# Forming two of the four weight sums of a seven-product pair by a DMA that adds in place, in a two-layer encoder on one core

## The chip, the core and the metric

The kernel runs on one core of a Trainium2 chip. A core has a matrix engine (PE, with PEld for its weight loads), a vector engine (DVE), an activation engine (ACT), a general engine (POOL), an engine that only issues transfers (SP), and 16 DMA engines that move data between the chip's main memory (HBM) and the on-chip buffer (SBUF). The five engines run their own instruction lists in order and wait for each other by semaphores. The metric is the device time of one execution in microseconds (us), lower being better, and it is quoted as the median of several runs.

## What is computed

Two layers of an encoder over 512 tokens of width 1024. Each layer has three parts, and every part adds to x:

```python
for l in range(DEPTH):                       # DEPTH = 2
    x = x + hybrid_mixer(rms_norm(x, ...), w_in[l], ...)          # two kinds of attention heads
    x = x + memory_cross_attention(rms_norm(x, ...), rms_norm(mem, ...), ...)
    x = x + conv_ffn(rms_norm(x, norm_ffn[l]), w_up[l], conv_w[l], conv_b[l], w_down[l])
return rms_norm(x, norm_final)

def conv_ffn(h, w_up, conv_w, conv_b, w_down):
    u = h @ w_up                             # 1024 -> 2 * 2816: a gate half and a value half
    ...                                      # width-3 depthwise convolution over positions
    gate, val = jnp.split(u, 2, axis=-1)
    return (jax.nn.silu(gate) * val) @ w_down
```

The change lies in `h @ w_up`.

## The kernel before, in words

**Numbers in two parts.** Every fp32 operand of a product is split into a rounded part (hi) and a rest (lo), and a product is three matmuls: hi·hi, hi·lo, lo·hi. ACT makes hi by a cast (`ACT.copy`), and POOL or DVE makes lo by a subtraction (`tensor_sub`). `operand_of` (L566) does this for one piece of a weight, 128 partitions by 512 columns.

**Seven products for eight.** The 22 column blocks of the gate half and the 22 of the value half belong together in 22 pairs. For pairs 7 to 21 of each layer, 30 pairs in all, the product of the 2x2 blocks is formed with seven block products in place of eight (`up`, L1604). The weight's blocks are 11, 12, 21 and 22, each 128 x 512 here: raw block A of the plan holds 11 (its first half) and 22 (its second half), raw block B holds 21 and 12. The seven left operands are 11, 12, 22 and four sums, which `combined` (L576) makes:

- s1 = 22 + 21 and s3 = 11 + 21, from the raw blocks;
- s2 = s3 + 22 and s4 = s2 + 12.

Each sum is one POOL `tensor_add` of 512 columns into a temporary `t`, and then one ACT cast and one DVE subtraction into a `hi` or `lo` weight tile. A `hi`-tagged tile here holds both parts of s1 or of s4, and a `lo`-tagged one both parts of s2 or of s3. The three plain blocks go into `r` tiles, also by one cast and one subtraction each. `up` uses the operands in the order 11, s1, 22 of the pair before, s2, 12, s4, s3. Between two pairs, `down_grouped` (L1672) takes one block of the down projection: 24 matmuls of 512 columns. The products of a pair are 84 matmuls of 256 columns.

**Loads.** All weights lie in HBM in the order of use. `emit_raw` (L563) has SP load the next block of 512 KB into one of three `raw` tiles; `get_w` keeps the loading and splitting ahead of the use.

**Buffers.** `wpool` holds the raw tiles and four tiles each of `hi` and `lo`. `tpool` holds 14 temporaries `t` of 2 KB per partition, which all stages share: softmax rows, rotary pieces, convolution outputs, sums of weights.

**Who sets the order.** The calls are not issued where they are written. They are recorded on a tape (`Taped`, `Tape`), and `Tape.plan` (L375) works out an order for each engine from a table of assumed costs (`Step`, L101), the buffers there are, and the order in which the calls were recorded. `Tape.play` then issues the calls (L404, which is why the profile puts nearly every instruction on that line). The planner lets a tile of a tag be opened ahead of those recorded before it only while more than a certain number of that tag's buffers are free: for `t` that number is 9 (`ASIDE`, L77, and `room`, L292). A DMA counts as 450 ns on the engine that issues it (L117).

**The first microseconds.** SP loads x and the first three weight blocks piece by piece, then three blocks of 512 KB (raw_114 to raw_116), two bias tables, the parameters, and then pieces of the memory tokens and further blocks. POOL makes the lo parts of raw_114, raw_116 and raw_122 there, DVE those of raw_115 and raw_119; between them POOL computes the inverse root of the first norm (`s_132`) and spreads it (`s_133`). PE needs `s_133` for a small matmul (`tr_139`) and the parts of raw_119 and raw_122 for the value projection (`mm_159`, `mm_160`).

Of the kernel before, what the change touches and what calls it, by code (L numbers as in the profile page):

```python
# [11 lines left out]
F32 = mybir.dt.float32  # L12
F32R = mybir.dt.float32r
AF = mybir.ActivationFunctionType
ALU = mybir.AluOpType
# [4 lines left out]
P = 128  # L20
# [6 lines left out]
KC = D // P  # L27
# [471 lines left out]
def encoder_kernel(ctx: ExitStack, tc: tile.TileContext, t: dict, out: list):  # L499
    nc = tc.nc  # L500
    tape = Tape()
    PE, ACT, DVE, POOL, SP = (
        Taped(tape, e, calls) for e, calls in zip(ENGINES, (nc.tensor, nc.scalar, nc.vector, nc.gpsimd, nc.sync)))
    late = Late(PE)
    LO_A, SUMS, LO_S = DVE, POOL, DVE
# [2 lines left out]
    xpool = ctx.enter_context(tc.tile_pool(name="xpool", bufs=1))  # L508
    wpool = ctx.enter_context(tc.tile_pool(name="wpool", bufs=N_W))
    rpool = ctx.enter_context(tc.tile_pool(name="rpool", bufs=23))  # L510
    tpool = ctx.enter_context(tc.tile_pool(name="tpool", bufs=14))
    spool = ctx.enter_context(tc.tile_pool(name="spool", bufs=24))
    psum = ctx.enter_context(tc.tile_pool(name="psum", bufs=2, space=PSUM))

# [2 lines left out]
    def nm(s):  # L517
        uid[0] += 1
        return f"{s}_{uid[0]}"

    def rtile(shape, dt=F32R):
        return rpool.tile([P, *shape], dt, tag="r", name=nm("r"), padded_shape=[P, *pad(shape)])

    def pad(shape):
        n = 1
        for s in shape[1:]:
            n *= s
        return [1024 // n, *shape[1:]]
# [6 lines left out]
    def tmp(shape=(S,)):  # L535
        return tpool.tile([P, *shape], F32, tag="t", name=nm("t"))
# [10 lines left out]
    f = lambda ap: ap.bitcast(F32)  # L547


    plan, raws, ready = [], [], []  # L550
# [3 lines left out]
    def raw_tile():  # L554
        key, src, nk, ncol, eng = plan[len(raws)]
        if eng[1:] == "x":
            raw = rtile((nk, ncol), F32)
        else:
            raw = wpool.tile([P, nk, ncol], F32, tag="raw", name=nm("raw"), bufs=N_RAW)
        raws.append(raw)  # L560
        return raw, src

    def emit_raw():  # L563
        SP.dma_start(*raw_tile())

    def operand_of(v, tile, sub):  # L566

        w = tile.rearrange("p (n k) c -> p n k c", n=2)
        ACT.copy(w[:, 0], v)
        sub.tensor_sub(w[:, 1], v, f(w[:, 0]))  # L570
        return [(w[:, 0, k], w[:, 1, k]) for k in range(4)]

    def wtile(tag):
        return wpool.tile([P, KC, P], F32R, tag=tag, name=nm(tag))

    def combined(first, second, early):  # L576

        parts = {}
        for n, v in (("11", first[:, 0:4]), ("12", second[:, 4:8]), ("22", first[:, 4:8])):
            parts[n] = operand_of(v, rtile((8, P)), LO_A)  # L580
        sums = {n: tmp((4, P)) for n in ("s3", "s1", "s2", "s4")}
        SUMS.tensor_add(sums["s1"], first[:, 4:8], second[:, 0:4])
        SUMS.tensor_add(sums["s3"], first[:, 0:4], second[:, 0:4])
        SUMS.tensor_add(sums["s2"], sums["s3"], first[:, 4:8])
        SUMS.tensor_add(sums["s4"], sums["s2"], second[:, 4:8])
        for n, tag in (("s1", "hi"), ("s2", "lo"), ("s4", "hi"), ("s3", "lo")):
            parts[n] = operand_of(sums[n], rtile((8, P)) if early else wtile(tag), LO_S)
        return parts

    def emit_split(act=ACT, cuts=2):  # L590
        n = len(ready)
        key, src, nk, ncol, eng = plan[n]
        raw = raws[n]
        if eng == "A":
            ready.append(raw)
            return
        if eng[0] == "B":
            ready.append(combined(raws[n - 1], raw, eng[1:] == "r"))
            raws[n - 1] = raws[n] = None
            return  # L600
        raws[n] = None
        if key[0] in ("up", "down", "memq", "memo"):
            cuts = 1
        if eng[1:] == "r":
            hi, lo = rtile((nk, ncol)), rtile((nk, ncol))
        else:
            hi = wpool.tile([P, nk, ncol], F32R, tag="hi", name=nm("hi"))
            lo = wpool.tile([P, nk, ncol], F32R, tag="lo", name=nm("lo"))
        for i in range(cuts):
            k = slice(nk * i // cuts, nk * (i + 1) // cuts)  # L610
            act.copy(hi[:, k], raw[:, k])
            (POOL if eng[0] == "P" else DVE).tensor_sub(lo[:, k], raw[:, k], f(hi)[:, k])
        ready.append((hi, lo))

    def get_w(key, ahead=AHEAD):
        n = done[0]
        assert plan[n][0] == key, (plan[n][0], key)
        ahead = n + 1 + ahead
        while ahead < min(len(plan), n + 1 + AHEAD_HELD) and plan[ahead][4][1:] == "r":
            ahead += 1  # L620
        while len(ready) < min(len(plan), ahead):
            while len(raws) < min(len(plan), len(ready) + N_RAW):
                emit_raw()
            emit_split()
        while len(raws) < min(len(plan), len(ready) + N_RAW):
            emit_raw()
        done[0] += 1
        w = ready[n]
        ready[n] = None
        return w  # L630
# [34 lines left out]
    first = nc.const_aps.tensor(0.0, (P, P), F32)  # L665
# [221 lines left out]
    for n in FIRST:  # L887
        if isinstance(n, (int, slice)):
            c, cs = (n, slice(0, S)) if isinstance(n, int) else (0, n)
            hi, lo, g = nn.hi[:, c, cs], nn.lo[:, c, cs], xg0[c][:, S : S + 1]  # L890
# [7 lines left out]
        k = slice(k0, k0 + nk)  # L898
# [12 lines left out]
    for l in range(DEPTH):  # L911
# [119 lines left out]
        parts = [None] * 8  # L1031
# [935 lines left out]
```

## Time and profile before

| | |
|---|---|
| median of 3 runs | 1303.92 us (1303.55 to 1304.28) |
| the profiled execution's own time | 1303.15 us |
| its span, first to last instruction | 1301.1 us |
| mean granted TensorE clock | 0.999 |
| PE busy | 1291.9 us, 99% of the span |
| DVE, ACT, POOL busy | 1066.1, 777.3, 655.8 us |
| DMA | 137.47 MB, a mean of 106 GB/s |

The span is what the profile covers; the execution's own time has 2.05 us more, which lie around it. A matmul's row in the profile lasts longer than the time until the next one starts, since matmuls overlap, so a PE that is busy all the time isn't shown to be at its peak by that alone: the distance between the starts of equal groups tells it. In the rows, `t<-raw,raw x2` is a group of two instructions that write a `t` tile from two `raw` tiles; the profile leaves the buffers' numbers out. "Idle before" is the idle time of the engine just before, with what ended it.

### The profile page before, as it was taken

What the parts mean: (1) busy time and instruction counts of PE and PEld (TensorE: products, weight loads), DVE (VectorE), ACT (ScalarE), POOL (GpSimd) and SP (SyncE); (2) the same over time, 40 slices, a digit from 0 to 9 for tenths busy, and PEclk for the clock granted to TensorE, in tenths of its full rate; (3) what the DMA queues carried; (4) which work ended last, traced back from release to release, by engine and by line L of the source; (5) the groups of instructions that cost most, each with busy time, mean ns of one, the idle gap of its engine ahead of it and who ended that gap; (6) DMA issues with size and microseconds to landing.
All of it is one profiled execution on the core that took longest, in us unless ns stands there. A gap on an engine that the chain in (4) does not pass through costs nothing.

```text
span 1301.1 us, 20672 instructions
## 1 busy us (share of the span) xinstructions
PE 1291.9 (99%) x7485; PEld 1135.6 (87%) x7485; DVE 1066.1 (82%) x1999; ACT 777.3 (60%) x1510; POOL 655.8 (50%) x523
## 2 busy tenths in 40 slices
PE   9999999999999999999999999999999999999998
PEld 8898888888889999999888988888888999999997
DVE  8679886768999998878655887866789998997784
ACT  7776686555565555555537867865655645554552
POOL 4565866716743334334626566765367224542260
PEclk9999999999999999999999999999999999999999
DMA  8651313313323333233356322232133233333231
GB/s 286 194 171 49 114 49 97 96 35 113 98 81 98 110 134 98 66 97 113 122 162 179 114 81 82 66 99 96 49 98 97 82 113 115 112 99 98 77 118 65
DMA packets 42901, 137.47 MB, mean 106 GB/s; under 512 B 5040, under 2 KB 8496, under 8 KB 42800
## 3 DMA queue, kind: packets, MB, share of 16 engines
q1 hardware_dynamic: 42224, 135.51, 33.3%
q8 instruction: 59, 0.97, 0.3%
q10 hardware_dynamic: 576, 0.66, 0.1%
q14 instruction: 42, 0.34, 0.1%
HBM read 126.18 MB, written 2.10 MB: 99 GB/s over the span
## 4 chain that ended last, share of the span: by engine, by line
PE 94%; POOL 1%; DVE 1%; issue 1%; ACT 1%; DMA 0%; SPq 0%; DVEq 0%; POOLq 0%
PE mm L404 55%; PE sc L404 20%; PE tr L404 20%; POOL lo L404 1%; ACT t L404 0%; POOL s L404 0%; DVE t L404 0%; DVE r L404 0%; DVE s L404 0%; DMA xT<-in_w 0%; ACT r L404 0%; POOL t L404 0%; DVE mm L404 0%; DVE sc L404 0%; POOL r L404 0%
## 5 line engine op out<-in xcount | busy, mean ns | idle before, releaser
L404 POOL TENSOR_TENSOR lo<-raw,hi 128x512 fp32r<-128x512 f32 (+2 forms) x168 | 265.8, 1599 | 185.8 <-ACT hi L404 179.9
L404 PE MATMUL mm<-xg,hi 128*128 128x512 f32 (+1 forms) x1026 | 319.3, 391 | 0.0
L404 POOL TENSOR_TENSOR t<-raw,raw 128x512 f32<-128x512 f32 x60 | 86.5, 1463 | 290.4 <-DMA raw<-in_w 213.8
L404 ACT CAST hi<-raw 128x512 fp32r<-128x512 f32 (+2 forms) x216 | 163.8, 784 | 111.8 <-PE mm L404 35.2
L404 PEld LDWEIGHTS mm<-xg,hi 128*128 128x128 f32 x1026 | 188.4, 188 | 35.5
L404 PE MATMUL mm<-xg,lo 128*128 128x512 f32 (+1 forms) x513 | 199.7, 389 | 0.0
L404 PE MATMUL mm<-r,hi 128*128 128x512 f32 (+1 forms) x608 | 192.0, 388 | 0.0
L404 PE MATMUL sc<-r,r 128*128 128x256 f32 (+1 forms) x736 | 131.8, 310 | 0.9 <-ACT t L404 0.9
L404 PEld LDWEIGHTS mm<-r,hi 128*128 128x128 f32 x608 | 111.9, 188 | 21.6 <-DVE xg L404 0.8
L404 PE MATMUL mm<-r,lo 128*128 128x512 f32 (+1 forms) x336 | 123.3, 367 | 0.0
L404 PEld LDWEIGHTS mm<-xg,lo 128*128 128x128 f32 x513 | 96.3, 188 | 20.2
L404 PEld LDWEIGHTS sc<-r,r 128*128 128x128 f32 x736 | 103.5, 191 | 7.4 <-ACT t L404 2.0
L404 PE MATMUL mm<-hi,xg 128*128 128x512 f32 (+1 forms) x384 | 108.1, 358 | 0.0
L404 PE MATMUL sc<-r,hi 128*128 128x256 f32 (+1 forms) x752 | 106.7, 288 | 0.0
L404 POOL TENSOR_SCALAR t<-t,s 128x512 f32<-128x512 f32 (+1 forms) x112 | 67.0, 613 | 71.8 <-DVE s L404 71.7
L404 POOL TENSOR_TENSOR t<-t,raw 128x512 f32<-128x512 f32 x60 | 99.5, 1658 | 4.7
L404 PEld LDWEIGHTS sc<-r,hi 128*128 128x128 f32 x752 | 97.0, 192 | 1.4
L404 PE MATMUL tr<-r,lo 128*128 128x256 f32 x720 | 96.2, 283 | 0.0
L404 PE MATMUL tr<-r,r 128*128 128x256 f32 x720 | 96.1, 283 | 0.0
L404 PEld LDWEIGHTS tr<-r,r 128*128 128x128 f32 x720 | 92.6, 191 | 2.3
L404 PEld LDWEIGHTS tr<-r,lo 128*128 128x128 f32 x720 | 90.7, 192 | 0.0
L404 ACT ACTIVATE t<-sc,s,s 128x512 f32<-128x512 f32 (+1 forms) x96 | 68.1, 711 | 29.2 <-DVE s L404 25.8
(158 smaller groups left out, 2756.3 us busy)
## 6 DMA issues: line engine op xcount, KB each, us to landing
raw<-in_w SPq DMA_DIRECT2D x207, 512.0 KB, 3.6
r<-r SPq DMA_DIRECT2D x30, 256.0 KB, 3.6
r<-in_bias SPq DMA_DIRECT2D x16, 384.0 KB, 4.6
raw<-in_w SPq DMA_DIRECT2D x8, 384.0 KB, 3.8
r<-in_memT SPq DMA_DIRECT2D x4, 512.0 KB, 7.2
xT<-in_w SPq DMA_DIRECT2D x7, 256.5 KB, 4.6
r<-in_w SPq DMA_DIRECT2D x9, 128.0 KB, 4.1
t<-in_memT SPq DMA_DIRECT2D x4, 256.0 KB, 6.1
```

Source lines behind the costliest of these rows:

```text
L404: call(*args, **kwargs)
```

## The change

The temporaries shrink from 14 to 10, and the space (8 KB per partition) holds two new tiles `acc` of 4 KB. For each pair, SP loads block A (11 and 22) from HBM a second time, into `acc`. Then POOL issues a DMA with `accum_op=ALU.add`, which reads block 21 from HBM twice and adds it to both halves of `acc`. After it `acc` holds s3 and s1. ACT casts the whole tile in one instruction of 1024 columns, DVE subtracts in one of 1024; s2 and s4 are still POOL's adds, s2 now from `acc`. The weight tiles are as many as before: one `hi` and one `lo` tile for s3 and s1 together, one `hi` for s2, one `lo` for s4.

```diff
-    tpool = ctx.enter_context(tc.tile_pool(name="tpool", bufs=14))
+    tpool = ctx.enter_context(tc.tile_pool(name="tpool", bufs=10))
...
+    accs = {}
+
     def emit_raw():
+        n = len(raws)
         SP.dma_start(*raw_tile())
+        if plan[n][4] == "B":
+            accs[n] = acc = wpool.tile([P, KC, P], F32, tag="acc", name=nm("acc"), bufs=2)
+            SP.dma_start(acc, plan[n - 1][1])
+            more = plan[n][1][:, 0:4].rearrange("p k c -> p (k c)").unsqueeze(1).to_broadcast([P, 2, 4 * P])
+            POOL.dma_start(acc.rearrange("p (n k) c -> p n (k c)", n=2), more, accum_op=ALU.add)
...
-    def combined(first, second, early):
+    def combined(first, second, acc):
...
-        sums = {n: tmp((4, P)) for n in ("s3", "s1", "s2", "s4")}
-        SUMS.tensor_add(sums["s1"], first[:, 4:8], second[:, 0:4])
-        SUMS.tensor_add(sums["s3"], first[:, 0:4], second[:, 0:4])
-        SUMS.tensor_add(sums["s2"], sums["s3"], first[:, 4:8])
-        SUMS.tensor_add(sums["s4"], sums["s2"], second[:, 4:8])
-        for n, tag in (("s1", "hi"), ("s2", "lo"), ("s4", "hi"), ("s3", "lo")):
-            parts[n] = operand_of(sums[n], rtile((8, P)) if early else wtile(tag), LO_S)
+        hi, lo = wtile("hi"), wtile("lo")
+        ACT.copy(hi, acc)
+        LO_S.tensor_sub(lo, acc, f(hi))
+        for i, n in enumerate(("s3", "s1")):
+            parts[n] = [(hi[:, 4 * i + k], lo[:, 4 * i + k]) for k in range(4)]
+        s2, s4 = tmp((4, P)), tmp((4, P))
+        SUMS.tensor_add(s2, acc[:, 0:4], first[:, 4:8])
+        SUMS.tensor_add(s4, s2, second[:, 4:8])
+        for n, v, tag in (("s2", s2, "hi"), ("s4", s4, "lo")):
+            parts[n] = operand_of(v, wtile(tag), LO_S)
         return parts
```

Since the planner orders everything anew, the change shows far from its own lines. Three places follow.

On POOL near the start of the program, before the change (rows 11 to 17; `lo_135` is the lo part of raw_116, `t_161` gathers squares of the memory tokens, `s_132` and `s_133` are the first norm's root and its spread form, `lo_150` is the lo part of raw_122):

```order
11 L404 TENSOR_TENSOR lo_118<-raw_114,hi_117 128x512 x2
12 L404 TENSOR_TENSOR lo_135<-raw_116,hi_134 128x512 x2
13 L404 TENSOR_TENSOR t_161<-t_161,t_171 128x512
14 L404 TENSOR_TENSOR s_132<-s_131,mhalf 128x4
15 L404 TENSOR_TENSOR s_133<-s_132,mask 128x16
16 L404 TENSOR_TENSOR t_161<-t_161,t_189 128x512
17 L404 TENSOR_TENSOR lo_150<-raw_122,hi_149 128x512 x2
```

and there now (`acc_838` and `acc_858` belong to the first two pairs, which PE multiplies some 350 us later):

```order
11 L404 TENSOR_TENSOR lo_118<-raw_114,hi_117 128x512 x2
12 L404 TENSOR_TENSOR lo_135<-raw_116,hi_134 128x512 x2
13 L404 DMA acc_838<-in_w 128x2x512
14 L404 DMA acc_858<-in_w 128x2x512
15 L404 TENSOR_TENSOR s_132<-s_131,mhalf 128x4
16 L404 TENSOR_TENSOR s_133<-s_132,mask 128x16
17 L404 TENSOR_TENSOR lo_150<-raw_122,hi_149 128x512 x2
```

Two DMA issues stand where one add stood ahead of `s_132`, and the add between `s_133` and `lo_150` has gone to a later place.

On SP at the same time, before (rows 30 to 35):

```order
30 L404 DMA gcol<-in_gcol 128x8
31 L404 DMA t_161<-in_memT 128x512
32 L404 DMA t_171<-in_memT 128x512
33 L404 DMA raw_119<-in_w 128x1024
34 L404 DMA t_189<-in_memT 128x512
35 L404 DMA raw_122<-in_w 128x1024
```

and now:

```order
30 L404 DMA gcol<-in_gcol 128x8
31 L404 DMA acc_838<-in_w 128x1024
32 L404 DMA acc_858<-in_w 128x1024
33 L404 DMA raw_119<-in_w 128x1024
34 L404 DMA t_161<-in_memT 128x512
35 L404 DMA raw_122<-in_w 128x1024
```

Ahead of raw_122 stand two loads of 512 KB in place of two of 256 KB; `t_171` and `t_189` are loaded later.

On PE, the first use of `lo_150` (a piece of the difference, - before and + now; `mm_159` and `mm_160` are two outputs of the value projection):

```order
 L404 MATMUL mm_159<-hi_149,xg_97 128x512
-L404 MATMUL mm_160<-hi_120,xg_97 128x512
-L404 MATMUL mm_160<-lo_121,xg_97 128x512
 L404 MATMUL mm_159<-lo_150,xg_97 128x512
 L404 MATMUL mm_159<-hi_149,xg_98 128x512
 L404 MATMUL mm_159<-hi_149,xg_97 128x512
-L404 MATMUL mm_160<-hi_120,xg_98 128x512
 L404 MATMUL mm_160<-hi_120,xg_97 128x512
 L404 MATMUL mm_159<-lo_150,xg_97 128x512
```

The first use of `lo_150` has come two matmuls nearer, since the two that stood ahead of it now follow. The small matmul `tr_139<-s_133,sel` likewise stands two matmuls earlier than before.

More of the change, by code (lines that the diff above doesn't have):

```diff
@@ L597, in emit_split @@
         if eng[0] == "B":
-            ready.append(combined(raws[n - 1], raw, eng[1:] == "r"))
+            ready.append(combined(raws[n - 1], raw, accs.pop(n)))
             raws[n - 1] = raws[n] = None
```

## The prediction

> **What bounds the kernel now.** I read the page first: busy times, transfer sizes, and the shares of the chain of work that ended last.
>
> ```profile
> span 1301.1 us, 20672 instructions
> PE 1291.9 (99%) x7485; PEld 1135.6 (87%) x7485; DVE 1066.1 (82%) x1999; ACT 777.3 (60%) x1510; POOL 655.8 (50%) x523
> ...
> PE 94%; POOL 1%; DVE 1%; issue 1%; ACT 1%; DMA 0%; SPq 0%; DVEq 0%; POOLq 0%
> ```
>
> PE is idle for 9.2 us of the span, and the chain runs through PE for 94% of it. POOL, which loses work by the change, is busy half the time and holds 1% of the chain. So I asked for busy time by stage: the first microseconds, the stage of the pairs (400 to 620 in the first layer), and the end.
>
> ```profile
> core 0: us, PE busy (x) PEld busy (x) DVE busy (x) ACT busy (x) POOL busy (x), PEclk, DMA share, GB/s
> 16.00:20.00 4.00, 4.00 (x19) 3.34 (x18) 3.44 (x7) 3.36 (x7) 1.00 (x1) 1.00 0.97 374
> 20.00:24.00 4.00, 4.00 (x19) 3.30 (x19) 3.94 (x4) 2.19 (x4) 4.00 (x3) 1.00 1.02 360
> 24.00:28.00 4.00, 4.00 (x20) 3.12 (x19) 3.69 (x11) 2.26 (x4) 3.45 (x4) 1.00 0.93 325
> 400.00:620.00 220.00, 220.00 (x1499) 205.04 (x1498) 195.86 (x309) 114.59 (x199) 83.09 (x54) 1.00 0.34 107
> 1250.00:1301.00 51.00, 45.20 (x313) 41.70 (x312) 29.95 (x69) 19.63 (x36) 16.29 (x10) 0.97 0.27 93
> ```
>
> Of the 9.2 us idle, 5.8 (51.00 less 45.20) lie in the last 51 us, which the change leaves as it was. 3.4 are left for everything else, and none lie in the pairs. Since busy is not yet peak, I measured the distance between equal places in neighbouring pairs, by the timeline of PE, with a stretch of single matmuls of 512 columns beside it.
>
> ```profile
> 33.84 0.39 PE L404 MATMUL mm<-lo,xg 128*128 128x512 f32 x1
> 34.07 0.39 PE L404 MATMUL mm<-hi,xg 128*128 128x512 f32 x1
> 34.30 0.39 PE L404 MATMUL mm<-lo,xg 128*128 128x512 f32 x1
> 34.52 0.62 PE L404 MATMUL mm<-hi,xg 128*128 128x512 f32 x2
> ...
> 506.18 0.63 PE L404 MATMUL mm<-xg,hi 128*128 128x512 f32 x2
> 513.08 1.60 PE L404 MATMUL sc<-r,hi 128*128 128x256 f32 x12
> 521.72 0.63 PE L404 MATMUL mm<-xg,hi 128*128 128x512 f32 x2
> 528.62 1.60 PE L404 MATMUL sc<-r,hi 128*128 128x256 f32 x12
> ```
>
> Three starts take 0.68 us, 0.227 for a matmul of 512 columns. A pair's period is 521.72 - 506.18 = 15.54 us, and the next place gives the same (528.62 - 513.08). It holds 24 matmuls of 512 columns (5.4 us) and 84 of 256 (10.1 us, 0.120 each, about half of 0.227). PE is at its pace there; nothing that other engines save can shorten it.
>
> **The change part by part.**
>
> *The pairs' sums.* The same pair on POOL and DVE, and then the groups of the stage:
>
> ```profile
> 503.95 2.87 POOL L404 TENSOR_TENSOR t<-raw,raw 128x512 f32<-128x512 f32 x2 [8.69 <-DVE t L404]
> 506.90 3.86 POOL L404 TENSOR_TENSOR t<-t,raw 128x512 f32<-128x512 f32 x2
> ...
> 513.21 0.68 DVE L404 TENSOR_TENSOR hi<-t,hi 128x512 fp32r<-128x512 f32 x1
> ```
>
> ```profile
> L404 POOL TENSOR_TENSOR t<-t,raw 128x512 f32<-128x512 f32 x26 | 43.4, 1669 | 2.0
> L404 POOL TENSOR_TENSOR t<-raw,raw 128x512 f32<-128x512 f32 x24 | 33.2, 1403 | 123.6 <-DMA raw<-in_w 80.7 <-DVE t L404 17.4 <-ACT t L404 11.3
> L404 DVE TENSOR_TENSOR hi<-t,hi 128x512 fp32r<-128x512 f32 x26 | 20.5, 789 | 1.8 <-ACT hi L404 1.8
> L404 DVE TENSOR_TENSOR lo<-raw,hi 128x1024 fp32r<-128x1024 f32 x14 | 19.5, 1391 | 0.0
> L404 DVE TENSOR_TENSOR lo<-t,lo 128x512 fp32r<-128x512 f32 x26 | 19.2, 743 | 0.0
> L404 ACT CAST hi<-t 128x512 fp32r<-128x512 f32 x25 | 15.5, 620 | 13.8 <-PE mm L404 11.1 <-POOL t L404 2.4 <-PE sc L404 0.3
> L404 ACT CAST hi<-raw 128x1024 fp32r<-128x1024 f32 x14 | 14.7, 1049 | 7.9 <-PE sc L404 7.2 <-DMA raw<-in_w 0.5
> ```
>
> Per pair POOL loses two adds of 1.40 us and keeps two (s2, s4) of 1.67, ACT exchanges two casts of 0.62 for one of 1.05, and DVE exchanges 0.79 + 0.74 for one of 1.39. That frees 2.8, 0.2 and 0.1 us. All of it is worth nothing: s1 is added from 503.95 on, its lo part is done at 513.89, and PE takes it at 528.62, 14.7 us later.
>
> *The pairs' transfers.* A pair loads 1.05 MB now and 2.10 MB after. At the 107 GB/s for a share of 0.34 above, 15.54 us move 1.66 MB; 1.05 more make the share 0.34 x 2.71/1.66 = 0.56. There is room. The accumulate's length is in no row of this kernel. Its lower bound is a plain load of 512 KB, 3.6 us here, its upper bound the same twice (the tile read and written), 7.2:
>
> ```profile
> raw<-in_w SPq DMA_DIRECT2D x207, 512.0 KB, 3.6
> ```
>
> I take 3.6, since its bytes from HBM are those of that row. Either lies inside the lead of s1 and s3: the tiles acc are two, so one is open about two periods (31 us) ahead of use, of which the base takes 4, and cast and subtraction with their queues some 7 (503.95 to 513.89 with the adds left out). About 20 us are left, so the pairs cost 0 at either bound. Issuing it on POOL is in no row; bounds are an issue of nothing and the 2.2 us after which POOL's saving of 2.8 would be nearly gone. I take 1 us, near POOL's smallest operation below (1.03); POOL is idle for more than half of the stage (83.09 of 220), so this costs 0 too.
>
> *The start.* Here something does stand close to its use. SP's issues and the times to landing of gcol (what the bases will stand behind) and of raw_122, the first of the four blocks issued from 24.69 on; then POOL, ACT and PE:
>
> ```profile
> 16.63 0.44 SPq L404 DMA_DIRECT2D gcol<-in_gcol  x1
> 24.69 8.47 SPq L404 DMA_DIRECT2D raw<-in_w  x4
> ...
> gcol<-in_gcol SPq DMA_DIRECT2D x1, 4.0 KB, 7.3
> ...
> raw<-in_w SPq DMA_DIRECT2D x1, 512.0 KB, 4.8
> ```
>
> ```profile
> 27.62 1.03 POOL L404 TENSOR_TENSOR s<-s,mhalf 128x4 f32<-128x4 f32 x1
> 28.73 0.31 POOL L404 TENSOR_TENSOR s<-s,mask 128x16 f32<-128x16 f32 x1
> 29.00 1.29 POOL L404 TENSOR_TENSOR t<-t,t 128x512 f32<-128x512 f32 x1
> 30.25 2.55 POOL L404 TENSOR_TENSOR lo<-raw,hi 128x512 fp32r<-128x512 f32 x2
> ...
> 27.00 1.14 ACT L404 CAST hi<-raw 128x512 fp32r<-128x512 f32 x2 [0.71 <-DMA raw<-in_w]
> 29.56 1.14 ACT L404 CAST hi<-raw 128x512 fp32r<-128x512 f32 x2 [0.88 <-PE mm L404]
> ...
> 29.52 0.29 PE L404 MATMUL tr<-s,sel 128*128 128x16 f32 x2
> 32.48 0.62 PE L404 MATMUL mm<-lo,xg 128*128 128x512 f32 x2
> ```
>
> raw_122 is issued at 24.69 and lands at 29.5. From its landing the first half of `lo_150` takes 2.07 us (landed 29.46, cast from 29.56, subtracted from 30.25 in 1.28, done at 31.53). PE's first use is the second matmul at 32.48, so 32.71; two matmuls earlier, as the change orders it, 32.25. The second half comes 1.28 later than the first and is used four matmuls (0.91) later, so it adds 0.37 to whatever the first half stalls.
>
> Now the loads. The DMA engines are at a share of 0.93 to 1.02 from 16 to 28 us, so a byte put ahead of raw_122 delays it. Two bases of 0.52 MB come in and two token pieces of 0.26 go later: +0.52 MB at the three windows' mean of 353 GB/s is 1.5 us, a landing at 31.0. gcol lands at 23.9 (16.63 + 7.3), the bases behind it at about 25.4 and 26.9. The two accumulates (1.05 MB, 3.0 us) are issued from POOL then, so while raw_119 and raw_122 are in flight. If they run wholly behind these, raw_122 lands at 31.0; if they are wholly served first, at 34.0; if two queues with data under way share evenly, half of the 3.0 us falls on raw_122, 32.5. I take the middle, since nothing in the trace prefers one queue. The stalls are then landing + 2.07 - 32.25 + 0.37: 1.2 us at 31.0, **2.7 at 32.5**, 4.2 at 34.0.
>
> [...] No run so far shows two such queues here.
>
> raw_119, 1.5 us late as well, is cast from 27.00 on (28.5 then), and PE takes it seven matmuls (1.6 us) ahead of `lo_150`, at 30.7 at the earliest: it holds. POOL's two issues replace an add of 1.29 ahead of `s_132`; with 1 us each `s_133` ends 0.7 later, at 29.7, while `tr_139` would come at 29.07, 0.03 after the old end of 29.04. That stall, 0.7 us, lies in the same wait as the larger one (PE then reaches `lo_150` later by just as much), so it adds nothing. If both issues took the upper 2.2 us it would be 3.1 and would replace the 2.7.
>
> *Ten temporaries for fourteen.* No row says what it costs; the planner has ordered the attention stages anew. PE's idle time outside the end is 3.4 us, so a better order gains at most that; I take the same as the bound of a loss, and 0 as the value, since the products are the same and PE stays the bound.
>
> *Sum.* 0 (pairs) + 2.7 (start) + 0 (attention) = +2.7 us. The profiled execution took 1303.15 us, its span 1301.1 and 2.05 around it: 1305.9. Against the median of the runs, 1303.92: **1306.6 us**.
>
> **The rivals.**
>
> - *The start hides it (not slower).* The accumulates stand behind the loads already queued and raw_122 lands at 31.0: +1.2, 1305.1. For it: the bases land only at 25.4 and 26.9, after raw_122 has been issued at 24.69. Against it: the share near 1.0. It decides when raw_122 lands before 31.5.
> - *A better order (faster).* `lo_150` isn't late, since the accumulates wait for bases that are themselves late, and the new order of attention, with the start's small waits, wins the 3.4 us: 1300.5. For it: PE's waits outside the end exist. Against it: no part of the change aims at them.
> - *The accumulate moves its bytes twice.* Then raw_122 lands at 34.0, +4.2: 1308.1. [...]
> - *The accumulate becomes the wait in the pairs (slower).* Rows of 2 KB added in place could be slow. Up to 20 us to landing it is hidden; at 25 us, seven times the 3.6 of a plain load, a tile acc is taken for 4 + 25 + 2.4 (cast and subtraction) and some 3 of queueing, 34.4 us, while two pairs need 31.1: (34.4 - 31.1)/2 = 1.65 us a pair, and for the 28 pairs after the first of each layer +46, 1350. For it: no such transfer has been seen here; against it: seven times.
> - *The change doesn't relieve POOL.* An issue of 2.2 us or more leaves POOL no freer than before. This changes nothing in the pairs, and at the start it is the 3.1 above: 1307.0, inside the forecast.
>
> **How the numbers follow.** A measurement of this kernel can tell about 0.2%, 2.6 us, from no change: faster means below 1301.3, slower above 1306.5. The forecast (raw_122 between 31.5 and 33.3, attention within 1 us) has 0.35; its centre lies on the edge, so 0.19 of it count as slower and 0.16 as the same. The hidden start has 0.25, the same. The better order has 0.17, faster; the bytes twice 0.14, slower; the wait in the pairs 0.09, slower. That makes faster 0.17, same 0.41, slower 0.42. The range leaves out the wait in the pairs (0.09) and half of the better order beyond its 3.4 (0.08): from 1300.5 (1303.92 - 3.4) to 1311.5 (1303.92 + 4.2 + 3.4).
>
> **What the changed profile would show.** Right: in the pairs a period of 15.54 us as before with DMA at about 0.56, POOL's `t<-raw,raw` gone; raw_122 to landing at 31.5 to 33.3 us; a PE idle of about 2.7 us between 29 and 36 released by POOL's `lo`; PE busy unchanged within 1 us, and its idle grown by 2 to 3. Wrong: a longer period or PE waits on `acc` in 400 to 620 (the wait in the pairs), no PE idle near 32 (the hidden start), or more than 2 us lost or won in 60 to 290 or 680 to 930 (the attention).

## The result and the profile after

| | before | after |
|---|---|---|
| median of 4 runs | 1303.82 us | 1319.78 us (1318.69 to 1320.81) |
| ratio | | 1.0123, 95% interval 1.0111 to 1.0135 |
| span of the profiled execution | 1301.1 us | 1319.0 us |

The change makes the kernel 16.0 us slower. The direction was that of the forecast, the size was six times as much, and the time lies outside the range.

The page of the kernel after: the busy times, the chain, and the accumulates' row among the transfers.

```profile
span 1319.0 us, 20776 instructions
...
PE 1298.1 (98%) x7485; PEld 1138.3 (86%) x7485; DVE 1051.7 (80%) x1969; ACT 776.0 (59%) x1480; POOL 590.3 (45%) x493
...
PE 91%; DVE 5%; issue 2%; ACT 1%; POOL 1%; DMA 0%; SPq 0%; DVEq 0%; ACTq 0%; POOLq 0%
...
acc<-in_w POOLq DMA_DIRECT2D x30, 512.0 KB, 5.9
```

POOL is busy 65.5 us less, which was the change's saving, and PE still takes longer. Its busy time has grown by 6.2 us although it has the same 7485 matmuls: somewhere it ran slower. Its idle time (span less busy time) has grown from 9.2 to 20.9 us. Busy time by stage shows where. A row has the stretch and its length in us, then the busy time of PE, PEld, DVE, ACT and POOL with the number of instructions, the granted TensorE clock, the share of the DMA engines and GB/s. First before, then after, the same three stretches of the start:

```profile
16.00:29.00 13.00, 13.00 (x59) 10.59 (x58) 12.03 (x22) 8.49 (x16) 9.37 (x8) 1.00 0.95 346
29.00:36.00 7.00, 7.00 (x33) 5.81 (x33) 5.15 (x8) 5.69 (x10) 3.80 (x4) 1.00 0.63 212
36.00:44.00 8.00, 8.00 (x41) 6.77 (x40) 7.79 (x18) 3.39 (x10) 0.00 (x0) 1.00 0.57 160
```

```profile
16.00:29.00 13.00, 13.00 (x59) 10.36 (x57) 10.29 (x21) 7.24 (x14) 7.77 (x5) 1.00 1.01 384
29.00:36.00 7.00, 0.26 (x2) 0.00 (x0) 0.49 (x1) 1.36 (x3) 1.95 (x2) 0.76 0.69 177
36.00:44.00 8.00, 7.28 (x20) 5.86 (x21) 5.42 (x9) 5.05 (x10) 3.05 (x4) 0.57 0.84 226
```

From 16 to 29 us PE does the same number of matmuls. Then it stands still for nearly all of seven us, and from 36 to 44 it does 20 matmuls in the time of 41, at a granted clock of 0.57. By 44 us it is 133 - 81 = 52 matmuls behind, at 0.195 us each (8.00/41) some 10 us. More than half of the loss has happened before the first pair is multiplied. The timeline of POOL, and PE's first row after the gap, name the cause:

```profile
25.54 1.37 POOL L404 DMA_DIRECT2D acc<-in_w  x1
34.05 1.24 POOL L404 DMA_DIRECT2D acc<-in_w  x1 [7.14 <-issue]
34.81 1.56 POOL L404 TENSOR_TENSOR s<-s,mhalf 128x4 f32<-128x4 f32 x1
36.45 0.22 POOL L404 TENSOR_TENSOR s<-s,mask 128x16 f32<-128x16 f32 x1
...
36.72 0.61 PE L404 MATMUL tr<-s,sel 128*128 128x16 f32 x2 [7.46 <-POOL s L404]
```

The first accumulate is issued at 25.54 in 1.37 us. The second stands still for 7.14 us, put down to "issue", which is a wait for nothing that the profile shows, and behind it on POOL's list stand `s_132` and `s_133`, for which PE waits 7.46 us. The transfers' own rows tell what the second accumulate waited for; the last number is the time from issue to landing. The first row below is the first accumulate alone, the second the weight block raw_122:

```profile
acc<-in_w POOLq DMA_DIRECT2D x1, 512.0 KB, 8.2
...
raw<-in_w SPq DMA_DIRECT2D x1, 512.0 KB, 4.8
```

25.54 + 8.2 = 33.7: the second accumulate goes 0.3 us after the first has landed. Its own base, issued at 19.07 and landed 7.1 later, had been there since 26.2. And raw_122, issued at 24.49, landed at 29.3, no later than before.

In the pairs the same two groups of PE as shown of before, from one pair to the next, and the stage's busy times:

```profile
504.21 0.63 PE L404 MATMUL mm<-xg,hi 128*128 128x512 f32 x2
...
519.75 0.63 PE L404 MATMUL mm<-xg,hi 128*128 128x512 f32 x2
```

```profile
400.00:620.00 220.00, 219.42 (x1498) 204.50 (x1497) 195.29 (x303) 116.31 (x192) 57.05 (x42) 1.00 0.61 165
```

The period is 15.54 us, unchanged, while the DMA share has gone from 0.34 to 0.61. Outside the start PE's idle time has grown by 4.2 us. Most of it lies in the attention stages, where it has risen (first before, then after) from 0.37 to 2.44 between 680 and 800 and from 0.96 to 1.81 between 60 and 150. Another 1.2 are two waits of 0.6 for ACT, at 461 and 1108, one in each layer's pairs:

```profile
60.00:150.00 90.00, 89.04 (x529) 77.37 (x529) 78.36 (x188) 64.77 (x156) 61.52 (x65) 1.00 0.35 106
...
680.00:800.00 120.00, 119.63 (x691) 104.12 (x690) 89.70 (x230) 86.14 (x208) 75.84 (x80) 1.00 0.41 121
```

```profile
60.00:150.00 90.00, 88.19 (x524) 76.11 (x523) 72.04 (x186) 65.10 (x161) 59.64 (x64) 1.00 0.43 132
...
680.00:800.00 120.00, 117.56 (x662) 101.21 (x661) 84.16 (x207) 77.38 (x185) 63.96 (x66) 1.00 0.45 131
```

### The profile page after: what moved, and what is told of

Read it like the earlier page. It is cut to its first block, busy times and chain, and to the rows that moved or that the text cites. A ratio compares the mean times of both kernels' runs of the same rounds, so it can differ in the third digit from the quotient of the medians.

```text
span 1319.0 us, 20776 instructions
## 1 busy us (share of the span) xinstructions
PE 1298.1 (98%) x7485; PEld 1138.3 (86%) x7485; DVE 1051.7 (80%) x1969; ACT 776.0 (59%) x1480; POOL 590.3 (45%) x493
## 3 DMA queue, kind: packets, MB, share of 16 engines
q1 hardware_dynamic: 46544, 151.24, 35.9%
## 4 chain that ended last, share of the span: by engine, by line
PE 91%; DVE 5%; issue 2%; ACT 1%; POOL 1%; DMA 0%; SPq 0%; DVEq 0%; ACTq 0%; POOLq 0%
PE mm L404 53%; PE tr L404 19%; PE sc L404 19%; DVE t L404 2%; DVE r L404 1%; DVE s L404 1%; ACT t L404 1%; POOL lo L404 1%; DVE lo L404 0%; DVE mm L404 0%; DMA xT<-in_w 0%; ACT r L404 0%; ACT hi L404 0%; DVE xT L404 0%; DVE sc L404 0%
## 5 line engine op out<-in xcount | busy, mean ns | idle before, releaser
L404 POOL DMA_DIRECT2D acc<-in_w x30 | 36.8, 1226 | 216.5 <-DVE t L404 58.7
L404 PE MATMUL mm<-hi,xg 128*128 128x512 f32 (+1 forms) x384 | 110.8, 364 | 0.9 <-DVE r L404 0.5
L404 PE MATMUL tr<-r,hi 128*128 128x256 f32 x600 | 92.7, 283 | 1.2 <-ACT t L404 1.2
L404 POOL TENSOR_TENSOR t<-acc,raw 128x512 f32<-128x512 f32 x30 | 46.9, 1563 | 101.3 <-DMA raw<-in_w 68.0
L404 PE MATMUL sc<-r,lo 128*128 128x256 f32 (+1 forms) x496 | 88.3, 286 | 0.0
L404 PEld LDWEIGHTS tr<-r,hi 128*128 128x128 f32 x600 | 82.9, 192 | 1.8 <-ACT t L404 1.6
L404 PEld LDWEIGHTS mm<-hi,xg 128*128 128x128 f32 x384 | 70.0, 192 | 11.4 <-DVE r L404 0.7
```

Of the source, the lines that this page charges most:

```text
L404: call(*args, **kwargs)
```

## The experiments

Theory: the second accumulate cannot be issued before the first has landed, and holds POOL's list with the norm's root behind it; that is the start's loss. The rest comes from ten temporaries, by the planner's new order of the attention. Rivals: the added transfers make the start's loads late; the accumulates cost in the pairs; any new order costs as much.

**Late: no transfer of the pairs at the start.**

```diff
             SP.dma_start(acc, plan[n - 1][1])
+            behind_step(len(tape.steps) - 1, len(tape.steps) - 2)
```

> Every copy of blocks 11 and 22 is ordered behind the load of its own block B, so no transfer of the pairs stands in the first microseconds; all else is as in the changed kernel. My theory, that the changed kernel loses its 10.5 us at the start because the second accumulate holds POOL's list ahead of the root of the norm: PE's wait at 29 us and the halved clock behind it are gone, 1319.8 - 10.5 = 1309, between 1307.5 and 1311, and what is left over the 1303.9 of before (about 5 us) lies in the attention and in the pairs. Rival, that the pairs pay most of it: still above 1315.

1319.41 us, ratio 1.0134 (1.0116 to 1.0153): the expected 1309 failed. The longest waits of PE (in all, how many, the longest):

```profile
PE tr L404 <- DVE s L404: 2.4, 1, 2.4
PE tr L404 <- DVE t L404: 1.9, 3, 0.9
...
```

POOL's wait is gone, but others stand in its place, all over the program. The new constraint made the planner order everything anew, so this kernel differs from the changed one in far more than was meant. It tells nothing about the theory, except that a re-planned order is itself an edit. The other kernels on the start can be compared: going by the tiles' names in the traces, they have the changed kernel's lists on every engine except for the accumulates (halves also moves some sums of the pairs), and hold has the lists of before with its own instructions added.

**Apart: only the second accumulate behind the lo part of raw_122.**

```diff
             POOL.dma_start(acc.rearrange(...), more, accum_op=ALU.add)
+            added.append(len(tape.steps) - 1)
+            if len(added) == 2:
+                behind_step(added[-1], p_subs[2])
```

> The bases of the first two pairs are loaded as early as in the changed kernel, and the first accumulate stands ahead of the root of the norm as there; only the second accumulate comes behind the lo part of raw_122 on POOL. My theory (the second accumulate cannot be issued until the first has landed, and holds what is behind it): the root starts at about 27, s_133 ends before 29, no wait of PE, 1309 to 1310. Rival 1 (the loaded DMA engines make base or parts late): PE waits as before at about 29 us, for a weight or for POOL, by 1 to 7 us. Rival 2 (any one DMA issue on POOL holds it for 8 us): s_133 after 34, 1318 to 1320.

1311.01 us, ratio 1.0062 (1.0046 to 1.0077). POOL at the start:

```profile
27.05 1.37 POOL L404 DMA_DIRECT2D acc<-in_w  x1 [1.34 <-DMA acc<-in_w]
28.11 1.39 POOL L404 TENSOR_TENSOR s<-s,mhalf 128x4 f32<-128x4 f32 x1
29.57 0.22 POOL L404 TENSOR_TENSOR s<-s,mask 128x16 f32<-128x16 f32 x1
...
35.48 1.28 POOL L404 DMA_DIRECT2D acc<-in_w  x1 [0.80 <-issue]
```

One accumulate ahead of the root holds it for about 1.1 us and no more. PE waits 1.5 us for DVE ahead of a small matmul at 26.91, behind a subtraction on DVE that took 1.77 us here and 0.68 in the changed kernel; why is open. The second accumulate again goes only when the first has landed (27.05 + 8.2 = 35.2).

**Plain: POOL's DMA copies and adds nothing** (the sum is left out).

```diff
-            POOL.dma_start(acc.rearrange(...), more, accum_op=ALU.add)
+            POOL.dma_start(acc.rearrange(...), more)
```

> The DMA on POOL copies block 21 over both halves of acc and adds nothing (the sum is left out); order, sizes and queues stay. If the hold of the second DMA is a matter of the add (read and write back in SBUF): it is issued at about 27, PE does not wait, about 1309. If any DMA of POOL of this size (256 rows of 2 KB) keeps the next one waiting until it has landed: POOL is held as in the changed kernel, until the first has landed, 5 to 8 us, 1315 to 1320. It also gives the landing time of a plain transfer of POOL against the 5.9 us of the accumulate.

1308.9 us (one run). POOL issues both at once, and a copy on its queue lands after 4.0 us where the accumulate takes 5.9:

```profile
25.85 1.62 POOL L404 DMA_DIRECT2D acc<-in_w  x2
27.49 1.05 POOL L404 TENSOR_TENSOR s<-s,mhalf 128x4 f32<-128x4 f32 x1
...
acc<-in_w POOLq DMA_DIRECT2D x30, 512.0 KB, 4.0
```

The two plain DMAs went in 1.62 us together; of the changed kernel's two adding ones with the same bytes the second stood for 7.14. But more than the add differs. The pages' rows of POOL's queue (packets, MB, share of the 16 DMA engines), first of the changed kernel, then of plain:

```profile
q0 software_dynamic: 8160, 15.73, 7.3%
...
q0 software_dynamic: 4320, 15.73, 3.6%
```

Over 30 DMAs these are 272 packets each against 144: the accumulate moves 256 rows of 2 KB, and 144 is the count of a base with its 128 rows of 4 KB (30 bases added 4320 packets to SP's queue, 46544 against 42224). So by its count the copy goes in 128 pieces of 4 KB, and this run does not tell the add from the number of pieces.

**Halves: each accumulate issued as two of 128 rows.**

```diff
+            for i in range(2):
+                POOL.dma_start(acc[:, 4 * i : 4 * i + 4], plan[n][1][:, 0:4], accum_op=ALU.add)
```

> Each accumulate is issued as two, of one half of acc each (128 rows of 2 KB), all else as in the changed kernel. If POOL issues one DMA at a time and waits for its landing: the four at the start stand one behind the other, the root of the norm comes only after three landings, PE waits longer than 7.5 us, above 1322. If it is a room for a number of rows (more than 256, fewer than 512): the second half is issued at once, the third or fourth waits for a landing, and the start costs about what it does now or less, 1312 to 1320.

1316.83 us (one run).

```profile
26.14 2.84 POOL L404 DMA_DIRECT2D acc<-in_w  x3 [0.30 <-DMA acc<-in_w]
32.93 0.88 POOL L404 DMA_DIRECT2D acc<-in_w  x1 [3.94 <-issue]
```

Three go at once, the fourth waits until the first has landed (26.14 + 6.5 = 32.6), and PE waits 5.7 us for the root behind it. So here it was not one at a time: 384 adding rows were issued without a wait, and the 128 that would have made them 512 stood for 3.94 us.

**Wide: the same bytes in 128 rows of 4 KB.**

```diff
+            POOL.dma_start(acc, plan[n][1], accum_op=ALU.add)
```

> The accumulate adds the whole of block B (21 and 12) to acc, so it moves the same 512 KB in 128 rows of 4 KB in place of 256 of 2 KB; the second half of the sum is then another one than the kernel needs. If what holds the second accumulate is a room for rows: it is issued about 1 us after the first, no wait of PE, about 1309 to 1310. If it is the bytes, or that only one such accumulate of this size is under way at a time: POOL is held until the first has landed, 8 us, 1318 to 1320.

1312.4 us (one run).

```profile
25.76 2.04 POOL L404 DMA_DIRECT2D acc<-in_w  x2
27.48 1.38 POOL L404 TENSOR_TENSOR s<-s,mhalf 128x4 f32<-128x4 f32 x1
...
acc<-in_w POOLq DMA_DIRECT2D x30, 512.0 KB, 5.5
```

Two accumulates of 512 KB go at once when each has half the rows, with no wait of PE at the start. So in these runs the rows decided and not the bytes: 1 MB went at once in 256 rows, and in the changed kernel's 512 it did not. Nor did the add alone hold the next one: with 128 pieces each, as here (2.04 us for both) and in plain (1.62), two went at once whether they added or not. Of its 8.8 us, 2.1 are a later wait of PE for a transfer near 80 us, with the clock at half behind it for some 3 us (mean clock of the execution 0.997, in plain 0.999).

**Moved: the changed kernel's order, two instructions moved.** The first two accumulates are taken out of the finished order and put behind the lo part of raw_122; every other row of every engine stays.

```diff
-        for i in self.plan():
+        for i in self.moved(self.plan()):
```

> The changed kernel's own order on every engine, word for word; only the first two accumulates are taken from ahead of the norm's root on POOL and put right behind the lo part of raw_122. The bases stay early. My theory (POOL's list held by the second accumulate costs the 10.5 us of the start): s_133 ends near 29, PE's idle at 29 us falls from 7.5 to under 1 and its clock stays at 1.00, 1319.8 - 10 = 1309.5, between 1308 and 1311. Rival (the accumulates' own transfers, 8 us long beside the loads, make the weights of the start late): PE waits for a weight after 29 us instead and it stays above 1314.

1310.95 us, ratio 1.0060 (1.0047 to 1.0074). POOL at the start, and PE's busy time:

```profile
26.68 1.04 POOL L404 TENSOR_TENSOR s<-s,mhalf 128x4 f32<-128x4 f32 x1 [0.69 <-DVE s L404]
27.79 0.22 POOL L404 TENSOR_TENSOR s<-s,mask 128x16 f32<-128x16 f32 x1
...
32.67 1.35 POOL L404 DMA_DIRECT2D acc<-in_w  x1
```

```profile
29.00:60.00 31.00, 31.00 (x157) 26.31 (x156) 20.16 (x49) 20.74 (x50) 17.49 (x18) 1.00 0.92 248
```

PE no longer waits, with the bases still loaded early and the accumulates still running at the start. The second one had not gone by 41, more than 8.3 us after the first, and there no wait of PE stands behind it. The place of two issues on POOL was worth 16.0 - 7.9 = 8.1 us by the medians, 11.0 by the two profiled spans (1319.0, the changed kernel's slowest run, and 1308.0, the fastest of moved). The two waits of 0.6 us for ACT in the pairs are gone as well.

**Hold: the kernel before, POOL occupied for 8 us.** No transfer is added and nothing planned anew.

```diff
+                tc.nc.gpsimd.memset(self.hold, 1.0)
+                for _ in range(11):
+                    tc.nc.gpsimd.tensor_add(self.hold, self.hold, self.hold)
```

> The kernel before in its own order, with a memset and eleven adds of 256 columns on a scratch tile put on POOL just ahead of the norm's root: some 7.5 us in which POOL does nothing useful, no transfer added, nothing planned anew. If POOL's list held for that long is the whole cause of the start's loss: PE waits about 7 us for s_133, its clock is halved behind that as in the changed kernel, and it takes 1303.1 + 8 to 10.5 = 1311 to 1313.5. If the transfers had a part in it: at most 7 us more and no halved clock, below 1310.

1313.84 us, ratio 1.0078 (1.0065 to 1.0091), +10.3 us. The adds on POOL, PE's wait, and the clock:

```profile
27.43 8.08 POOL L406 TENSOR_TENSOR hold<-hold 128x256 f32<-128x256 f32 x11
35.46 1.03 POOL L409 TENSOR_TENSOR s<-s,mhalf 128x4 f32<-128x4 f32 x1
```

```profile
PE tr L409 <- POOL s L409: 7.1, 1, 7.1
```

```profile
29.00:36.00 7.00, 0.75 (x4) 0.28 (x2) 0.00 (x0) 1.14 (x2) 6.29 (x11) 0.81 0.32 107
36.00:44.00 8.00, 7.16 (x26) 5.86 (x27) 5.50 (x9) 4.88 (x9) 4.42 (x5) 0.74 0.30 103
```

A wait of 7.1 us costs 10.3 by the medians and 9.3 by the spans (1310.4 and 1301.1), with the clock at half behind it. That is about the start's loss of the changed kernel, without any of its transfers.

**Ten and twelve temporaries in the kernel before.**

```diff
-    tpool = ctx.enter_context(tc.tile_pool(name="tpool", bufs=14))
+    tpool = ctx.enter_context(tc.tile_pool(name="tpool", bufs=10))
```

> The kernel before with ten temporaries in place of 14 and nothing else; the sums are POOL's adds as before. Theory A, that the 5 us that the changed kernel loses outside the start come from the planner's order of the attention stages with ten temporaries: 1307 to 1309, with PE's loss in 60 to 150 and 720 to 860 as in the changed kernel. Theory B, that they come from the accumulates (POOL held, more transfers): 1303 to 1304.5.

> The kernel before with twelve temporaries. If fewer temporaries cost by their number, it lies between the kernel before and the one with ten: 1305 to 1307 under theory A. If what counts is that each new order of the planner's is another draw, it may lie anywhere from 1302 to 1310, out of order with the one of ten. Under theory B it is 1303 to 1304.5.

Ten: 1308.41 us, ratio 1.0038 (1.0026 to 1.0051). Twelve: 1310.26, ratio 1.0055 (1.0042 to 1.0068). With ten, PE waits where the changed kernel's PE waits outside the start. PE's longest wait in all and a stretch of the second layer's attention, first of moved, then of ten temporaries:

```profile
PE mm L404 <- DVE t L404: 2.2, 4, 0.8
```

```profile
680.00:800.00 120.00, 117.10 (x666) 100.50 (x665) 86.23 (x216) 81.54 (x197) 71.10 (x74) 1.00 0.40 121
```

```profile
PE mm L404 <- DVE t L404: 2.2, 4, 0.8
...
680.00:800.00 120.00, 117.12 (x665) 100.49 (x665) 87.00 (x219) 81.75 (x198) 71.98 (x75) 1.00 0.40 123
```

The same four waits of 2.2 us in all, the same 2.9 us of idle PE, and in the kernel with ten there is no accumulate at all. By the spans ten temporaries cost 5.5 us, of which 3.3 are idle time of PE and 2.2 more busy time (1294.1 against 1291.9); where the busy time lies is open. Twelve loses no less than ten (the medians differ by 1.9 us, the intervals overlap), and in other places (two waits of 1.8 us for ACT near 384 and 1031), so the loss does not follow the count.

**Aside: the rule for t scaled to ten buffers** (on top of moved).

```diff
-ASIDE = {"mm": 1, "r": 9, "t": 9, "s": 9}
+ASIDE = {"mm": 1, "r": 9, "t": 5, "s": 9}
```

> The kernel with the moved accumulates, planned with a t tile let ahead of its turn while more than 5 of the 10 are free, as it was more than 9 of the 14 before (with ten buffers the rule of 9 asks for all ten). If the rule is what spoils the order of the attention: 1304 to 1306. If the number of temporaries or the accumulates do it: 1308 to 1311.

1310.07 us, ratio 1.0051 (1.0037 to 1.0065), not told apart from moved. It trades the four waits for one of 3.0 us at 25 and one of 1.9 at 82. So the rule bears on where PE waits, but scaling it does not win the loss back.

**Thirteen, and 14 with another order.** The second is the kernel before with `"t": 10` in ASIDE.

> The kernel before with 13 temporaries. If the 5 to 7 us of ten and twelve are the price of fewer buffers, one fewer costs little: 1303 to 1305. If any newly planned order costs about that, because the order of before is an unusually good one: 1306 to 1311.

> The kernel before with all its 14 temporaries, planned with a t tile let ahead of its turn only while more than 10 are free, not 9: another order with the same buffers. If the number of temporaries is what costs: 1303 to 1304.5, as before. If the draw of the order is: 1306 to 1311.

Thirteen: ratio 1.0048 (1.0036 to 1.0060), some 6 us. Fourteen in another order: 1304.45 us, ratio 1.0006 (0.9997 to 1.0015), not told apart from before. So another order as such need not cost anything, and even one buffer fewer did. Three kernels with fewer and no other change lose 5 to 7 us each, in no order of their number. That fewer buffers force worse orders fits this; one other order with 14 is too few to rule out chance.

## Why the prediction was wrong

- *What bounds the kernel*: right. PE is the bound, and POOL's 65.5 us are worth nothing.
- *The pairs*: right. The period is 15.54 us as said, the DMA share 0.61 where 0.56 was worked out, and the accumulate's 5.9 us lie between the bounds of 3.6 and 7.2. The lead covers it; the two waits of 0.6 us in the pairs are not for `acc`.
- *The start, the step that failed*: "with 1 us each `s_133` ends 0.7 later". An issue alone takes 1.2 to 1.4 us, inside the bounds. But the bound of 2.2 us was set for an issue by itself, and the second one stood for 7.1 us more until the first had landed. `s_133` ended at 36.7 and not at 29.7. That two accumulates might not be issued one behind the other was in no row of before and among none of the rivals. The plain bound was at hand: the second issue cannot be shown to go before the first lands, 3.6 to 7.2 us later by the prediction's own numbers.
- *raw_122 late by the added bytes*: wrong in both parts. It landed at 29.3 and not 32.5. The bases' 0.52 MB cost it nothing: a share of 0.93 to 1.02 had been read as full, yet from 16 to 29 us the DMA engines moved 384 GB/s where they had moved 346, which is 0.49 MB more. And the accumulate came too late to share with it. Issued at 25.54, it moved its first packet at 28.9 (3.3 us later; 1.9 in the pairs), and only 6 of its 272 packets before 29.3. That two queues with data under way share evenly, on which 32.5 and with it the forecast's 2.7 us rest, no run shows: in the start's trace the two hardly overlapped before raw_122 had landed (those 6 packets), and what PE waited for instead was `s_133`, 7.46 us.
- *A stall costs its own length* (taken for granted): wrong. The 7.46 us of PE's wait cost some 10, since matmuls ran at half the clock behind it. In the slices of the changed kernel the clock is 1.00 up to 32 us, 0.50 from 33 to 42, and 1.00 again from 43:

```profile
31.00:32.00 1.00, 0.00 (x0) 0.00 (x0) 0.00 (x0) 0.00 (x0) 0.00 (x0) 1.00 1.10 221
...
33.00:34.00 1.00, 0.00 (x0) 0.00 (x0) 0.00 (x0) 0.00 (x0) 0.00 (x0) 0.50 0.59 221
...
42.00:43.00 1.00, 1.00 (x4) 0.80 (x3) 0.99 (x2) 0.97 (x3) 0.00 (x0) 0.53 1.05 395
43.00:44.00 1.00, 1.00 (x6) 0.83 (x5) 0.95 (x3) 0.99 (x3) 0.00 (x0) 1.00 0.91 350
```

  PE stopped at 29.3, the clock fell at 32.7 (0.85 in the slice from 32 to 33), and it came back after 6.2 us of work (36.7 to 42.9); in hold it came back after 3.2 (36.8 to 40.1, worked out from the 0.74 between 36 and 44). Shorter waits were followed by it as well. In late a wait of 2.4 us, the row below, was followed by half the clock from 28 to 34 us (0.43 us from one start of a 512-column matmul to the next, 0.23 after it), and in wide the wait of 2.1 by some 3 us of it; behind the 1.5 us in apart the clock was 1.00 from 29 to 44.

```profile
28.04 0.61 PE L404 MATMUL tr<-s,sel 128*128 128x16 f32 x2 [2.40 <-DVE s L404]
```
- *Ten temporaries*: mis-sized. Taken at 0 with a loss of at most 3.4, measured 5.4. The bound had no reason: the idle time that exists limits what an order can win, not what it can lose.

The sum as measured: 8.1 (POOL held) + 5.4 (ten temporaries) + 2.5 = 16.0. The 2.5 us are what moved has over the kernel with ten temporaries; their intervals touch, the two spans differ by 1.4, and what is in them is left open. The split is rough: with the 10.3 us of hold for the start, 0.3 would be left.

## What to carry to other kernels

An instruction that may block belongs on an in-order engine behind what others wait for, however short its issue; here the place of two DMA issues cost 8.1 us, more than all the adds they removed could have given (PE had 3.4 us of idle time outside the end). When a buffer is taken away, price what the planner loses by it with a run of that alone. And a wait of a matrix engine is to be priced with the slower clock behind it: here the profiled executions whose longest wait was 2.1 us or more (wide 2.1, late 2.4, aside 3.0, halves 5.7, hold 7.1, the changed kernel 7.5) had a mean clock of 0.995 to 0.997, against 0.999 before. Of twelve temporaries' two waits of 1.8 one stood in a stretch at 1.00 and one in a stretch at 0.99, and the 1.5 of apart came with 0.999.

## What the runs showed of the hardware

- POOL issued three adding DMAs of 128 rows in a row, and the fourth stood for 3.94 us (halves). The second of two of 256 rows stood for 7.14 us (the changed kernel); the second of two of 128 rows of 4 KB did not (wide, 2.04 us for both issues), nor that of two plain ones that went in 128 pieces of 4 KB (plain, 1.62 us). The held one went when the first had landed: at 34.05 against 33.7 (the changed kernel), 35.48 against 35.2 (apart) and 32.93 against 32.6 (halves). Whether plain DMAs of 512 pieces in all would be held too was not run.
- With the same 128 pieces of 4 KB, 512 KB landed after 5.5 us adding (wide) and after 4.0 plain; 256 adding rows of 2 KB landed after 5.9. Adding kept the DMA engines busy about twice as long for the same bytes in the same pieces: 7.0% of the span (wide) against 3.6% (plain).
- From 16 to 29 us DMA engines at a share of 0.95 moved 346 GB/s, and at 1.01 they moved 384, 11% more; so the share near 1 was no proof of a full path.
